# One UV tile for both halves of a paired chunk solve, and the chunk-end decay multiplied into the transposed keys

## The chip, the cores and the metric

One core of one Trainium2 chip. The metric is the device time of one execution in microseconds: the time from launch to end on that core. PE is TensorE, DVE is VectorE, ACT is ScalarE, POOL is GpSimd, SP is SyncE, whose queue only issues transfers.

## The reference, cut to what matters

One layer of a hybrid decoder, for a prompt of 2048 tokens and, with the same weights, for a decode step of 8 sequences by 4 tokens. One input projection feeds two token mixers; their gated outputs are merged and go through an output projection and a layer norm. The change is in the first mixer, a delta-rule recurrence with a state of 64x64 for each of 16 heads:

```python
def _rwkv7_recurrence(s0, r, w, k, v, kk, a):
    def step(s, inp):
        r_t, w_t, k_t, v_t, kk_t, a_t = inp
        s_kk = jnp.einsum('nhvk,nhk->nhv', s, kk_t)
        s = (s * w_t[:, :, None, :] - s_kk[..., None] * (kk_t * a_t)[:, :, None, :]
             + v_t[..., None] * k_t[:, :, None, :])
        return s, jnp.einsum('nhvk,nhk->nhv', s, r_t)
    xs = tuple(jnp.swapaxes(t, 0, 1) for t in (r, w, k, v, kk, a))
    s, y = lax.scan(step, s0, xs)
    return s, jnp.swapaxes(y, 0, 1)
...
    y_a = _norm(y_a, A_GN_EPS).reshape(n, t, A_WIDTH).astype(dt) * gn_a_gain + gn_a_bias
    o_a = (y_a + bonus.astype(dt)) * jax.nn.silu(z_a)
```

## The kernel before, in words

The prompt is cut into four segments of 512 tokens. In a segment the loop runs over four groups `h`, and a group holds two pairs of heads (`P0`, `P1`: a pair's 128 channels fill the partitions, 64 for each head). The large work is the projections: weight blocks `ww` against the segment's activations `uh` and `ul` (a high and a low part), matmuls `pp<-uh,ww` and `pp<-ul,ww` of 128x512 on PE, and the output projection `pp<-ww,mh` and `pp<-ww,ml`. The decode step is computed within the segment behind the second one.

A pair's 512 tokens are two halves of 256, and a half has C = 4 chunks of 64. `half` calls `prep`, which makes the tiles of a half: `AR` (scaled kk and r), `BK` (scaled a*kk and k), `UV` (for each head the values in one half of the partitions, and the state, later -U, in the other), `BT` (the transpose of `BK`, through a PSUM tile `sm`: the matmuls `sm<-cst,BK`), `W` (masked products of `BK` and `AR`, `sm<-AR,BK`), and `PL`, the decay of the state over a whole chunk (one number for each chunk and row). The step list `ORDER` has a `J` for each pair: first half, then `solve`, then second half. So one `solve` takes two halves together, the second half of one pair and the first half of the next, which do not depend on each other: 31 solves are of two halves and 2 of a single one (132 chunk steps, 124 of them paired).

`solve` inverts a triangular matrix for all chunks (tiles `ZX`, `HH`, `bdH`, `bdZ` in fp16, result `Z`), and then walks the four chunks in sequence. A chunk step is:

- X products, `ch<-UV,W` of 128x64: state and values against `W`; ScalarE copies X out (`tn<-ch`, the tile `xs`).
- Decayed state: ScalarE multiplies the state by `PL` (`tn<-UV,PL`, the tile `pst`), four instructions in a paired step (two heads by two halves).
- U products, `ch<-tn,Z`, and behind them in one bundle the first part of the output, `yy<-UV,AR`.
- Negation of U into `UV`, over the state that the two steps before have read: for each half one ScalarE instruction (head 0) and one VectorE instruction (head 1), `UV<-ch`.
- State products, `ch<-UV,BT` (S), and behind them in one bundle the second part of the output, `yy<-UV,W`.
- State update on VectorE: `UV[c+1] = S * PL + pst`, four scalar_tensor_tensor instructions (`UV<-ch,PL,tn`); at the last chunk the update goes to the state tile `sc`.

X, U and S lie in one PSUM tile `ch`, the output in `yy`. A bundle is a list of matmuls that PE does without anything between them.

No instruction is placed by hand. Each operation is recorded with its tiles by a helper (all rows of the profile have its line, L529, so the text goes by tile names), and a planner (`schedule`) fixes the order on each engine before the run: it keeps estimated durations (`cost`) and free tiles for each engine and always lets the engine that can start first take its next operation, by priority. On PE, `choose` prefers to stay with large matmuls or with small ones for some time (constants `STAY` 0.5 and `RUN` 2), since a change of shape costs time. The planner also keeps VectorE instructions with two inputs in SBUF and GpSimd instructions apart. The number of buffers of the tiles of a half is `JBN`, in the order `AR`, `W`, `UV`, `BT`, `Z`.

Of the kernel before, what the change touches and what calls it, by code (L numbers as in the profile page):

```python
# [25 lines left out]
C = JT // 64  # L26
# [38 lines left out]
DOFF = 0  # L65
JBN = 3, 2, 2, 2, 2
JB=dict(zip(("AR", "W", "UV", "BT", "Z"), JBN))
# [759 lines left out]
class Mixer:  # L827
# [227 lines left out]
    def ahead(self, n, g):  # L1055

        new = lambda tag: self.jb.tile([128, 512], F32R, tag=tag, name="w0", bufs=JB[tag])
        blk = FIRST[n]
        kw = {}
        if n == 2:  # L1060
            t = self.jb.tile([128, 2, 512], F32R, tag="W", name="w0", bufs=JB["W"])
            kw = dict(hi=t[:, 0], lo=t[:, 1])
        elif n == 3:
            kw = dict(hi=new("AR"), lo=new("BT"))
        elif n == 4:
            kw = dict(hi=new("UV"), lo=self.fx(dt=F32R))
        if not kw:
            if g == 0:
                self.wfirst[n] = self.ww.tile([128, 2, 2, 512], F32R, tag="ww", name="ww")
            kw = dict(hi=self.wfirst[n][:, g, 0], lo=self.wfirst[n][:, g, 1])  # L1070
        self.first[blk, g] = self.split(self.i["wf"][blk, g], **kw)
        if g == 0 and n > 2:
            self.early[blk] = (self.ch, self.yy)[n - 3].tile([128, 512], F32, tag=("ch", "yy")[n - 3], name="pp")
# [150 lines left out]
    def prep(self, s, p, j, slot, r, k, v, kn, g, lw):  # L1224
# [22 lines left out]
        self.act(P, cu, AF.Exp, scale=-0.5 * CDEC)  # L1247
        PL = self.jb.tile([128, C], F32, tag="PL", name="PL")
        G.tensor_copy(out=PL, in_=P[:, :, 64])
# [23 lines left out]

        UV = self.jb.tile([128, C, 2, 64], F32, tag="UV", name="UV", bufs=JB["UV"])
        ps = self.ps()
        pv = ps[:, 0:JT].rearrange("p (q t) -> p q t", q=2)
        self.pl.reserve = (UV,)
        for q in range(2):
            T.transpose(out=pv[:, q], in_=v2[:, q * 128:(q + 1) * 128], identity=self.ident)
        for e in range(2):  # L1280
            for h in range(2):
                A.copy(out=UV[64 - h * 64:128 - h * 64, e::2, h, :], in_=pv[e * 64:e * 64 + 64, :, h * 64:h * 64 + 64])

        ps = self.ps().rearrange("p (c t) -> p c t", c=C)
        for c in range(C):
            T.transpose(out=ps[:, c], in_=BK[:, c], identity=self.ident)
        BT = self.jb.tile([128, C, 128], F32, tag="BT", name="BT", bufs=JB["BT"])
        A.copy(out=BT, in_=ps)

# [4 lines left out]
        with self.pl.bundle():  # L1294
            for c in range(C):
                for h in range(2):
                    T.matmul(pw[h][:, c], lhsT=BK[HS[h], c], rhs=AR[HS[h], c], start=True, stop=True)
        B16, Bl, D = self.B16, self.bd["L"], slice(slot * C, (slot + 1) * C)
        for h in range(2):
# [4 lines left out]
            self.A.copy(out=W[R, h, :, 0:64], in_=AR[R, :, 0:64])  # L1304
        self.turns.append((p, AR, W, UV, BT, PL, bv, g[:, cs]))

    def half(self, s, p, j, ins):

        if not self.turns:
            self.B16 = self.j1.tile([128, 2 * C, 64], F16, tag="B16", name="B16")  # L1310
        self.prep(s, p, j, len(self.turns), *ins)

    def solve(self):
# [3 lines left out]
        ps_, self.turns = self.turns, []  # L1317
        Q = range(len(ps_))
        N = len(Q) * C
        B16, Bl, MB = self.B16[:, 0:N], self.bd["L"], self.bd["M"]  # L1320
# [54 lines left out]
        for c in range(C):  # L1375
            cp = self.ch.tile([128, 512], F32, tag="ch", name="ch").rearrange("p (k q t) -> p k q t", k=4, q=2)
            X, U, S = (cp[:, i, 0:len(Q)] for i in range(3))
            with self.pl.bundle():
                for q in Q:
                    p, AR, W, UV, BT, PL = ps_[q][:6]  # L1380
                    for h in range(2):
                        T.matmul(X[HS[h], q], lhsT=W[:, h, c, 0:64], rhs=UV[:, c, h], start=True, stop=True)
            xs = self.tiny(128).rearrange("p (q t) -> p q t", q=2)[:, 0:len(Q)]
            A.copy(out=xs, in_=X)
            pst = self.tiny(128).rearrange("p (q t) -> p q t", q=2)
            for q in Q:
                p, AR, W, UV, BT, PL = ps_[q][:6]
                for h in range(2):
                    R = HS[h]
                    self.act(pst[R, q], UV[R, c, h], AF.Copy, scale=PL[R, c:c + 1])  # L1390
            with self.pl.bundle():
                for q in Q:
                    for h in range(2):
                        T.matmul(U[HS[h], q], lhsT=Z[HS[h], q * C + c], rhs=xs[HS[h], q], start=True, stop=True)
                for q in Q:
                    p, AR, W, UV, BT, PL = ps_[q][:6]
                    for h in range(2):
                        T.matmul(Y[HS[h], q * C + c], lhsT=AR[HS[h], c, 64:128], rhs=UV[HS[h], c, h], start=q == 0, stop=False)
            for q in Q:
                UV = ps_[q][3]  # L1400
                self.act(UV[HS[0], c, 0], U[HS[0], q], AF.Copy, scale=-1.0)
                V.tensor_scalar(out=UV[HS[1], c, 1], in0=U[HS[1], q], scalar1=-1.0, scalar2=None, op0=MUL)
            with self.pl.bundle():
                for q in Q:
                    p, AR, W, UV, BT, PL = ps_[q][:6]
                    for h in range(2):
                        T.matmul(S[HS[h], q], lhsT=BT[:, c, HS[h]], rhs=UV[:, c, h], start=True, stop=True)
                for q in Q:
                    p, AR, W, UV, BT, PL = ps_[q][:6]
                    for h in range(2):  # L1410
                        T.matmul(Y[HS[h], q * C + c], lhsT=W[:, h, c, 64:128], rhs=UV[:, c, h], start=False, stop=q == len(Q) - 1)
            for q in Q:
                p, AR, W, UV, BT, PL = ps_[q][:6]
                if c < C - 1:
                    for h in range(2):
                        R = HS[h]
                        V.scalar_tensor_tensor(out=UV[R, c + 1, h], in0=S[R, q], scalar=PL[R, c:c + 1], in1=pst[R, q],
                                               op0=MUL, op1=ADD)
                else:
                    V.scalar_tensor_tensor(out=self.sc[:, p], in0=S[:, q], scalar=PL[:, c:c + 1], in1=pst[:, q],  # L1420
                                           op0=MUL, op1=ADD)
        yn = [self.groupnorm(Y[:, q * C:(q + 1) * C], C) for q in Q]
# [5 lines left out]
        for q in Q:  # L1428
            p, bv, g = ps_[q][0], *ps_[q][6:]
            t = self.t3()  # L1430
# [15 lines left out]
    def decode(self):  # L1446
# [94 lines left out]
        A.copy(out=BT, in_=ps)  # L1541
        UV = self.jb.tile([128, 8, 64], F32, tag="UV", name="UV", bufs=JB["UV"])
        self.pl.hold = self.pl.ops[-1]
# [496 lines left out]
```

## Time and profile before

| | us |
|---|---|
| median of 3 runs | 3134.05 |
| lowest, highest | 3130.12, 3137.01 |
| the profiled execution | 3128.51 |
| its span in the trace | 3126.7 |
| mean granted clock of TensorE, as a share of full speed | 0.969 |

The span runs from the first to the last instruction in the trace; the execution's time is 1.8 us longer. A time of this kernel compares with the median, and a sum over rows of the trace with the profiled execution.

### The profile page before, as it was taken

What the parts mean: (1) busy time and instruction counts of PE and PEld (TensorE: products, weight loads), DVE (VectorE), ACT (ScalarE), POOL (GpSimd) and SP (SyncE); (2) the same over time, 40 slices, a digit from 0 to 9 for tenths busy, and PEclk for the clock granted to TensorE, in tenths of its full rate; (3) what the DMA queues carried; (4) which work ended last, traced back from release to release, by engine and by line L of the source; (5) the groups of instructions that cost most, each with busy time, mean ns of one, the idle gap of its engine ahead of it and who ended that gap; (6) DMA issues with size and microseconds to landing.
All of it is one profiled execution on the core that took longest, in us unless ns stands there. A gap on an engine that the chain in (4) does not pass through costs nothing. (4 is left out here: it accounts for less than half of the span.)

```text
span 3126.7 us, 63842 instructions
## 1 busy us (share of the span) xinstructions
PE 2896.4 (93%) x24700; PEld 2332.8 (75%) x24700; DVE 1919.9 (61%) x4748; ACT 1566.2 (50%) x3859; POOL 1048.3 (34%) x1451
## 2 busy tenths in 40 slices
PE   8999999989989999989998788999999989998996
PEld 5777778768888989879774466777787766777675
DVE  3566676666576365565665575565676675566666
ACT  4466755656436455453541045554555346454652
POOL 4554456433252131222210242232232442334232
PEclk9999999999999999999998789999999999999997
DMA  8564556534362433425344432333343452533321
GB/s 303 199 229 161 175 191 222 191 127 160 117 226 99 130 108 112 137 94 178 136 128 150 158 110 97 135 124 122 131 152 124 156 176 79 172 119 122 108 83 38
DMA packets 132792, 451.86 MB, mean 145 GB/s; under 512 B 30500, under 2 KB 41636, under 8 KB 92680
## 3 DMA queue, kind: packets, MB, share of 16 engines
q0 software_dynamic: 33120, 241.19, 22.5%
q1 hardware_dynamic: 99368, 206.58, 19.6%
q8 instruction: 195, 3.19, 0.4%
q14 instruction: 109, 0.89, 0.1%
HBM read 345.83 MB, written 101.88 MB: 143 GB/s over the span
## 5 line engine op out<-in xcount | busy, mean ns | idle before, releaser
L529 PE MATMUL pp<-uh,ww 128*128 128x512 f32 (+1 forms) x5152 | 1476.8, 366 | 43.8 <-DMA ww<-wc_wf 15.6
L529 PEld LDWEIGHTS pp<-uh,ww 128*128 128x128 f32 x5152 | 880.5, 190 | 168.3 <-DVE t L529 22.7
L529 PE MATMUL pp<-ul,ww 128*128 128x512 f32 (+1 forms) x2576 | 883.7, 364 | 0.1
L529 PEld LDWEIGHTS pp<-ul,ww 128*128 128x128 f32 x2576 | 468.6, 190 | 54.5 <-issue 1.4
L529 POOL DMA_DIRECT2D ww<-wc_wf x190 | 109.0, 574 | 625.3 <-PE pp L529 514.5
L529 POOL TENSOR_TENSOR ww<-fx,ww 128x512 fp32r<-128x512 f32 x178 | 234.4, 1330 | 211.5 <-ACT ww L529 197.7
L529 ACT CAST ZX<-sm 128x512 f16<-128x512 f32 (+1 forms) x363 | 206.3, 572 | 91.0 <-PE sm L529 86.7
L529 ACT ACTIVATE tn<-UV,PL 64x64 f32<-64x64 f32 x512 | 177.0, 346 | 117.9 <-DVE UV L529 95.8
L529 POOL TENSOR_TENSOR t<-t,t 128x256 fp32r<-128x256 f32 (+2 forms) x160 | 150.6, 943 | 199.5 <-ACT t L529 189.1
L529 DVE TENSOR_TENSOR HH<-sm,lev 128x512 f16<-128x512 f32 (+1 forms) x165 | 111.3, 674 | 160.5 <-PE sm L529 159.7
L529 PE MATMUL pp<-ww,mh 128*128 128x256 f32 x960 | 190.4, 290 | 3.5 <-ACT zt L529 1.9
L529 DVE TENSOR_SCALAR UV<-ch 64x64 f32<-64x64 f32 x256 | 55.2, 227 | 207.3 <-ACT UV L529 184.4
L529 POOL TENSOR_TENSOR tn<-tn,mhalf 128x4 f32<-128x4 f32 (+2 forms) x108 | 100.9, 935 | 216.1 <-DVE tn L529 214.1
L529 PE MATMUL pp<-ww,uh 128*128 128x256 f32 x1024 | 171.6, 291 | 1.4 <-DVE t L529 0.8
L529 ACT CAST bdZ<-sm 64x512 f16<-64x512 f32 (+1 forms) x264 | 149.5, 566 | 24.9 <-PE sm L529 20.1
L529 PEld LDWEIGHTS pp<-ww,mh 128*128 128x128 f32 x960 | 154.9, 193 | 8.0 <-ACT zt L529 2.3
L529 PEld LDWEIGHTS pp<-ww,uh 128*128 128x128 f32 x1024 | 140.7, 190 | 5.3 <-ACT UV L529 0.7
L529 DVE SCALAR_TENSOR_TENSOR UV<-ch,PL,tn 64x64 f32<-64x64 f32 x384 | 108.7, 283 | 57.4 <-PE ch L529 47.5
L529 ACT ACTIVATE t<-pp 128x512 f32<-128x512 f32 (+1 forms) x160 | 80.6, 519 | 118.3 <-PE pp L529 100.7
L529 PE MATMUL pp<-ww,ml 128*128 128x256 f32 x480 | 138.4, 289 | 0.1
L529 ACT ACTIVATE UV<-ch 64x64 f32<-64x64 f32 x256 | 51.6, 215 | 171.3 <-PE yy L529 137.8
L529 DVE COPY bdH<-HH 64x512 f16<-64x512 f16 (+1 forms) x396 | 124.7, 315 | 8.5
(255 smaller groups left out, 5420.1 us busy)
## 6 DMA issues: line engine op xcount, KB each, us to landing
ww<-wc_wf POOLq DMA_DIRECT2D x190, 1024.0 KB, 5.1
wc_wf<-ww SPq DMA_DIRECT2D x65, 1024.0 KB, 5.4
fx<-in_wf SPq DMA_DIRECT2D x140, 256.0 KB, 3.4
ww<-wc_wv POOLq DMA_DIRECT2D x24, 1024.0 KB, 5.2
ww<-wc_wo POOLq DMA_DIRECT2D x16, 1024.0 KB, 5.1
wa<-in_wa SPq DMA_DIRECT2D x16, 512.0 KB, 5.2
wc_wv<-ww SPq DMA_DIRECT2D x8, 1024.0 KB, 5.5
fx<-in_wo SPq DMA_DIRECT2D x32, 256.0 KB, 2.8
```

Of the source, the lines that this page charges most:

```text
L529: op.fn = lambda: real(*[res(x) for x in a], **{k: res(x) for k, x in kw.items()})
```

## The change

It has four parts.

- `UV` and `PL` are no longer made for each half: `half` makes one tile of each for the two halves of a solve, `[128, 2, C, 2, 64]` and `[128, 2, C]`, and `prep` fills its slot. One `UV` tile takes the place of two (`JBN` 2 to 1). In the decode step the tile that was called `UV` comes from another pool, and so does one early weight block that borrowed the space.
- In `prep`, behind the products of `BK` and `AR`, VectorE multiplies `BK` in place by `PL` (128x512, one instruction a half). The transposes to `BT` are moved behind that, so that `BT` holds the decay.
- In `solve` the decayed state `pst` is made by VectorE, one 64x128 product for each head and both halves. The negation of U is one ScalarE and one VectorE instruction for both halves. The state update is then S + `pst`, one 64x128 addition for each head.
- With a single half the same instructions have 64 columns.

```diff
-JBN = 3, 2, 2, 2, 2
+BKG = 0
+PSG = 0
+JBN = 3, 2, 1, 2, 2
...
         elif n == 4:
-            kw = dict(hi=new("UV"), lo=self.fx(dt=F32R))
+            if g == 0:
+                self.wfirst[n] = self.jb.tile([128, 2, 512], F32R, tag="UV", name="w0", bufs=JB["UV"])
+            kw = dict(hi=self.wfirst[n][:, g], lo=self.fx(dt=F32R))
...
-        PL = self.jb.tile([128, C], F32, tag="PL", name="PL")
+        PL = self.PL[:, slot]
         G.tensor_copy(out=PL, in_=P[:, :, 64])
...
-        UV = self.jb.tile([128, C, 2, 64], F32, tag="UV", name="UV", bufs=JB["UV"])
+        UV = self.UV[:, slot]
...
-        self.pl.reserve = (UV,)
+        if slot == 0:
+            self.pl.reserve = (self.UV,)
...
-        ps = self.ps().rearrange("p (c t) -> p c t", c=C)
-        for c in range(C):
-            T.transpose(out=ps[:, c], in_=BK[:, c], identity=self.ident)
-        BT = self.jb.tile([128, C, 128], F32, tag="BT", name="BT", bufs=JB["BT"])
-        A.copy(out=BT, in_=ps)
...
                     T.matmul(pw[h][:, c], lhsT=BK[HS[h], c], rhs=AR[HS[h], c], start=True, stop=True)
+        (G if BKG else V).tensor_tensor(out=BK, in0=BK, in1=PL.unsqueeze(2).broadcast_to([128, C, 128]), op=MUL)
+        ps = self.ps().rearrange("p (c t) -> p c t", c=C)
+        for c in range(C):
+            T.transpose(out=ps[:, c], in_=BK[:, c], identity=self.ident)
+        BT = self.jb.tile([128, C, 128], F32, tag="BT", name="BT", bufs=JB["BT"])
+        A.copy(out=BT, in_=ps)
...
         if not self.turns:
             self.B16 = self.j1.tile([128, 2 * C, 64], F16, tag="B16", name="B16")
+            self.UV = self.jb.tile([128, 2, C, 2, 64], F32, tag="UV", name="UV", bufs=JB["UV"])
+            self.PL = self.jb.tile([128, 2, C], F32, tag="PL", name="PL")
...
+        UVs, PLs = self.UV[:, 0:len(Q)], self.PL[:, 0:len(Q)]
...
-            pst = self.tiny(128).rearrange("p (q t) -> p q t", q=2)
-            for q in Q:
-                p, AR, W, UV, BT, PL = ps_[q][:6]
-                for h in range(2):
-                    R = HS[h]
-                    self.act(pst[R, q], UV[R, c, h], AF.Copy, scale=PL[R, c:c + 1])
+            pst = self.tiny(128).rearrange("p (q t) -> p q t", q=2)[:, 0:len(Q)]
+            for h in range(2):
+                R = HS[h]
+                (G if PSG else V).tensor_tensor(out=pst[R], in0=UVs[R, :, c, h],
+                                                in1=PLs[R, :, c:c + 1].broadcast_to([64, len(Q), 64]), op=MUL)
...
-            for q in Q:
-                UV = ps_[q][3]
-                self.act(UV[HS[0], c, 0], U[HS[0], q], AF.Copy, scale=-1.0)
-                V.tensor_scalar(out=UV[HS[1], c, 1], in0=U[HS[1], q], scalar1=-1.0, scalar2=None, op0=MUL)
+            self.act(UVs[HS[0], :, c, 0], U[HS[0]], AF.Copy, scale=-1.0)
+            V.tensor_scalar(out=UVs[HS[1], :, c, 1], in0=U[HS[1]], scalar1=-1.0, scalar2=None, op0=MUL)
...
-            for q in Q:
-                p, AR, W, UV, BT, PL = ps_[q][:6]
-                if c < C - 1:
-                    for h in range(2):
-                        R = HS[h]
-                        V.scalar_tensor_tensor(out=UV[R, c + 1, h], in0=S[R, q], scalar=PL[R, c:c + 1], in1=pst[R, q],
-                                               op0=MUL, op1=ADD)
-                else:
-                    V.scalar_tensor_tensor(out=self.sc[:, p], in0=S[:, q], scalar=PL[:, c:c + 1], in1=pst[:, q],
-                                           op0=MUL, op1=ADD)
+            if c < C - 1:
+                for h in range(2):
+                    R = HS[h]
+                    V.tensor_tensor(out=UVs[R, :, c + 1, h], in0=S[R], in1=pst[R], op=ADD)
+            else:
+                for q in Q:
+                    V.tensor_tensor(out=self.sc[:, ps_[q][0]], in0=S[:, q], in1=pst[:, q], op=ADD)
```

Since the planner places every operation anew, the order on all engines changes. Over the whole program PE turns between large matmuls (128x256 and 128x512) and all others 2713 times before, 2601 times with the change; PE has the same number of matmuls. Three places on PE follow. In the rows a matmul is named by output<-inputs, its shape and how many stand in a row.

The first place is a paired chunk step in the middle of the program, from the U products to the next X products. Before:

```order
L529 MATMUL ch<-tn,Z 64x64 x4
L529 MATMUL yy<-UV,AR 64x64 x4
L529 MATMUL pp<-uh,ww 128x512 x2
L529 MATMUL ch<-UV,BT 64x64 x4
L529 MATMUL yy<-UV,W 64x64 x4
L529 MATMUL pp<-ul,ww 128x512
L529 MATMUL pp<-uh,ww 128x512 x2
L529 MATMUL pp<-ul,ww 128x512
L529 MATMUL ch<-UV,W 64x64 x4
```

With the change:

```order
L531 MATMUL ch<-tn,Z 64x64 x4
L531 MATMUL yy<-UV,AR 64x64 x4
L531 MATMUL pp<-ul,ww 128x512
L531 MATMUL pp<-uh,ww 128x512
L531 MATMUL ch<-UV,BT 64x64 x4
L531 MATMUL yy<-UV,W 64x64 x4
L531 MATMUL pp<-uh,ww 128x512
L531 MATMUL pp<-ul,ww 128x512
L531 MATMUL pp<-uh,ww 128x512
L531 MATMUL ch<-UV,W 64x64 x4
```

Two large matmuls stand between the U and the S products as before; between the S products and the next X products there are three instead of four.

The second place is the end of the decode step's state products, `sm<-d,BT`, where `d` is a temporary tile of the decode step (its number tells the tiles apart). Before:

```order
L529 MATMUL sm<-d_21554,BT 64x256 x2
L529 MATMUL sm<-d_21567,BT 64x256 x2
L529 MATMUL sm<-d_21574,BT 64x256 x2
...
L529 MATMUL sm<-d_21627,BT 64x256 x2
L529 MATMUL sm<-cst,t_20695 128x128 x2
L529 MATMUL sm<-d_21637,BT 64x256 x2
L529 MATMUL sm<-d_21657 32x32 x4
```

With the change:

```order
L531 MATMUL sm<-d_21184,BT 64x256 x2
L531 MATMUL pp<-uh,ww 128x512 x2
L531 MATMUL pp<-ul,ww 128x512
L531 MATMUL pp<-uh,ww 128x512 x2
L531 MATMUL pp<-ul,ww 128x512
L531 MATMUL sm<-d_21209,BT 64x256 x2
L531 MATMUL pp<-uh,ww 128x512 x2
L531 MATMUL pp<-ul,ww 128x512
L531 MATMUL sm<-d_21219,BT 64x256 x2
```

The last state products stood in a row of their own and now stand between large matmuls. In the whole stretch from the first of them to `sm<-d 32x32` there are 42 large matmuls before and 158 with the change, the last 61 of them behind the last state product.

The third place is in the last paired solve of the program. Before, one chunk step from its S products on:

```order
L529 MATMUL ch<-UV,BT 64x64 x4
L529 MATMUL yy<-UV,W 64x64 x4
L529 MATMUL pp<-ww,mh 128x256
L529 MATMUL pp<-ww,ml 128x256
L529 MATMUL pp<-ww,mh 128x256 x2
L529 MATMUL pp<-ww,ml 128x256
L529 MATMUL pp<-ww,mh 128x256 x2
L529 MATMUL pp<-ww,ml 128x256
L529 MATMUL pp<-ww,mh 128x256
L529 MATMUL ch<-UV,W 64x64 x4
```

With the change, from the S products of its first step on:

```order
L531 MATMUL ch<-UV,BT 64x64 x4
L531 MATMUL yy<-UV,W 64x64 x4
L531 MATMUL pp<-ww,ml 128x256
L531 MATMUL pp<-ww,mh 128x256
L531 MATMUL ch<-UV,W 64x64 x4
L531 MATMUL ch<-tn,Z 64x64 x4
L531 MATMUL yy<-UV,AR 64x64 x4
L531 MATMUL ch<-UV,BT 64x64 x4
L531 MATMUL yy<-UV,W 64x64 x4
L531 MATMUL ch<-UV,W 64x64 x4
```

From the second step on the small matmuls follow each other with nothing between, and the last half's `sm<-AR,BK`, which stood behind this solve, stands ahead of these steps.

## Rows read from the trace of the kernel before

**Rows 1.** The page: busy time, share of the span and instructions of each engine.

```profile
PE 2896.4 (93%) x24700; PEld 2332.8 (75%) x24700; DVE 1919.9 (61%) x4748; ACT 1566.2 (50%) x3859; POOL 1048.3 (34%) x1451
```

**Rows 2.** Groups by shape: busy us, mean ns, idle before, what ended it.

```profile
L529 PE MATMUL ch<-UV,W 128*64 128x64 f32 x1024 | 60.4, 235 | 11.9 <-DVE UV L529 4.5 <-ACT W L529 3.0
...
L529 PE MATMUL ch<-UV,BT 128*64 128x64 f32 x1024 | 59.2, 235 | 36.4 <-DVE UV L529 34.6 <-ACT UV L529 1.4
```

**Rows 3.** Waits: who waited for whom, us in total, times, longest.

```profile
DVE UV L529 <- ACT UV L529: 184.4, 180, 2.6
...
PE ch L529 <- DVE UV L529: 39.1, 97, 1.3
...
PE sm L529 <- DVE BK L529: 19.6, 6, 11.1
```

**Rows 4.** Timeline of one paired chunk step: start us, us, work, idle before.

```profile
1919.00 0.45 PE L529 MATMUL ch<-UV,W 128*64 128x64 f32 x8
...
1920.58 0.45 PE L529 MATMUL ch<-tn,Z 64*64 64x64 f32 x8
...
1920.86 0.40 PE L529 MATMUL yy<-UV,AR 64*64 64x64 f32 x8
...
1921.23 0.22 ACT L529 ACTIVATE UV<-ch 64x64 f32<-64x64 f32 x1 [0.97 <-PE yy L529]
...
1921.48 0.23 DVE L529 TENSOR_SCALAR UV<-ch 64x64 f32<-64x64 f32 x1 [2.54 <-ACT UV L529]
...
1921.81 0.22 ACT L529 ACTIVATE UV<-ch 64x64 f32<-64x64 f32 x1 [0.35 <-DVE UV L529]
1922.05 0.23 DVE L529 TENSOR_SCALAR UV<-ch 64x64 f32<-64x64 f32 x1 [0.34 <-ACT UV L529]
...
1922.34 0.45 PE L529 MATMUL ch<-UV,BT 128*64 128x64 f32 x8 [0.41 <-DVE UV L529]
...
1922.84 1.23 DVE L529 SCALAR_TENSOR_TENSOR UV<-ch,PL,tn 64x64 f32<-64x64 f32 x4 [0.56 <-PE ch L529]
...
1924.21 0.45 PE L529 MATMUL ch<-UV,W 128*64 128x64 f32 x8 [0.28 <-DVE UV L529]
```

**Rows 5.** Groups by shape on ScalarE and VectorE: instructions that go, and nearest prices.

```profile
L529 ACT ACTIVATE tn<-UV,PL 64x64 f32<-64x64 f32 x512 | 177.0, 346 | 117.9 <-DVE UV L529 95.8 <-POOL PL L529 9.6 <-POOL t L529 2.0
...
L529 DVE SCALAR_TENSOR_TENSOR UV<-ch,PL,tn 64x64 f32<-64x64 f32 x384 | 108.7, 283 | 57.4 <-PE ch L529 47.5
...
L529 DVE TENSOR_TENSOR W<-sm,cst 128x512 f32<-128x512 f32 x129 | 84.8, 679 | 16.2 <-PE sm L529 15.8
...
L529 ACT COPY UV<-sm 64x128 f32<-64x128 f32 x256 | 66.4, 260 | 20.9 <-PE sm L529 17.6
...
L529 DVE TENSOR_TENSOR t<-t,t 128x512 f32<-128x512 f32 x24 | 19.2, 800 | 0.5
...
L529 DVE TENSOR_TENSOR d<-d,roped 64x128 f32<-64x128 f32 x4 | 1.1, 286 | 0.1
```

**Rows 6.** Timeline of PE: large matmuls and eight small ones between them.

```profile
2059.50 0.39 PE L529 MATMUL pp<-uh,ww 128*128 128x512 f32 x1
2059.73 0.41 PE L529 MATMUL sm<-HH,bdZ 128*128 128x64 f16 x8
2059.97 0.48 PE L529 MATMUL pp<-uh,ww 128*128 128x512 f32 x1
2060.29 0.39 PE L529 MATMUL pp<-ul,ww 128*128 128x512 f32 x1
```

**Rows 7.** Timeline of PE: the decode step's state products, first row and what follows.

```profile
1671.58 0.38 PE L529 MATMUL sm<-d,BT 64*64 64x256 f32 x1
...
1709.92 0.61 PE L529 MATMUL sm<-d 128*32 128x32 f32 x8 [4.89 <-DVE d L529]
```

**Rows 8.** Windows: length; busy (x) of PE, PEld, DVE, ACT, POOL; PEclk, DMA, GB/s.

```profile
1690.00:1700.00 10.00, 5.26 (x22) 1.73 (x24) 5.90 (x17) 0.00 (x0) 0.00 (x0) 0.60 0.63 215
1700.00:1710.00 10.00, 4.50 (x20) 1.51 (x17) 7.38 (x23) 2.36 (x8) 0.00 (x0) 0.50 0.48 165
```

More of the change, by code (lines that the diff above doesn't have):

```diff
@@ L1304, in prep @@
             self.A.copy(out=W[R, h, :, 0:64], in_=AR[R, :, 0:64])
-        self.turns.append((p, AR, W, UV, BT, PL, bv, g[:, cs]))
+        self.turns.append((p, AR, W, UV, BT, bv, g[:, cs]))
     def half(self, s, p, j, ins):
@@ L1379, in solve @@
                 for q in Q:
-                    p, AR, W, UV, BT, PL = ps_[q][:6]
+                    p, AR, W, UV, BT = ps_[q][:5]
                     for h in range(2):
@@ L1395, in solve @@
                 for q in Q:
-                    p, AR, W, UV, BT, PL = ps_[q][:6]
+                    p, AR, W, UV, BT = ps_[q][:5]
                     for h in range(2):
                         T.matmul(Y[HS[h], q * C + c], lhsT=AR[HS[h], c, 64:128], rhs=UV[HS[h], c, h], start=q == 0, stop=False)
-            for q in Q:
-                UV = ps_[q][3]
-                self.act(UV[HS[0], c, 0], U[HS[0], q], AF.Copy, scale=-1.0)
-                V.tensor_scalar(out=UV[HS[1], c, 1], in0=U[HS[1], q], scalar1=-1.0, scalar2=None, op0=MUL)
+            self.act(UVs[HS[0], :, c, 0], U[HS[0]], AF.Copy, scale=-1.0)
+            V.tensor_scalar(out=UVs[HS[1], :, c, 1], in0=U[HS[1]], scalar1=-1.0, scalar2=None, op0=MUL)
             with self.pl.bundle():
                 for q in Q:
-                    p, AR, W, UV, BT, PL = ps_[q][:6]
+                    p, AR, W, UV, BT = ps_[q][:5]
                     for h in range(2):
@@ L1408, in solve @@
                 for q in Q:
-                    p, AR, W, UV, BT, PL = ps_[q][:6]
+                    p, AR, W, UV, BT = ps_[q][:5]
                     for h in range(2):
                         T.matmul(Y[HS[h], q * C + c], lhsT=W[:, h, c, 64:128], rhs=UV[:, c, h], start=False, stop=q == len(Q) - 1)
-            for q in Q:
-                p, AR, W, UV, BT, PL = ps_[q][:6]
-                if c < C - 1:
-                    for h in range(2):
-                        R = HS[h]
-                        V.scalar_tensor_tensor(out=UV[R, c + 1, h], in0=S[R, q], scalar=PL[R, c:c + 1], in1=pst[R, q],
-                                               op0=MUL, op1=ADD)
-                else:
-                    V.scalar_tensor_tensor(out=self.sc[:, p], in0=S[:, q], scalar=PL[:, c:c + 1], in1=pst[:, q],
-                                           op0=MUL, op1=ADD)
+            if c < C - 1:
[5 more added lines that the diff above has]
+                    V.tensor_tensor(out=self.sc[:, ps_[q][0]], in0=S[:, q], in1=pst[:, q], op=ADD)
         yn = [self.groupnorm(Y[:, q * C:(q + 1) * C], C) for q in Q]
@@ L1428, in solve @@
         for q in Q:
-            p, bv, g = ps_[q][0], *ps_[q][6:]
+            p, bv, g = ps_[q][0], *ps_[q][5:]
             t = self.t3()
@@ L1541, in decode @@
         A.copy(out=BT, in_=ps)
-        UV = self.jb.tile([128, 8, 64], F32, tag="UV", name="UV", bufs=JB["UV"])
+        UV = self.t5((128, 8, 64))
         self.pl.hold = self.pl.ops[-1]
```

## The prediction

> **What bounds the kernel now.** I read the engines' busy shares first, then the groups by shape, then the waits, and last two stretches of the timeline. The shares [rows 1] make PE the bound: busy 2896.4 us, 93% of the span, with VectorE at 61% and ScalarE at 50%. So only two things can shorten the span: time in which PE's queue stands at a matmul whose input is late, and time lost when PE turns from one shape to another. The change touches the chunk chain, four small steps per solve that run beside the large projections. Of its matmuls the state products (`ch<-UV,BT`) have 36.4 us of PE idle in front of them, 34.6 of it for VectorE's `UV`; the next chunk's first products (`ch<-UV,W`) have 11.9, of which 4.5 for that reason [rows 2]. The waits agree: 39.1 us in 97 waits of `ch` for VectorE's `UV`, the largest sum on PE itself, and VectorE in turn sat 184.4 us behind ScalarE's `UV` [rows 3].
>
> One paired chunk step shows why [rows 4]. The U products start at 1920.58. Then ScalarE negates U of the first half at 1921.23, VectorE at 1921.48, ScalarE the second half's at 1921.81, VectorE at 1922.05: four instructions strictly in turn, although they write disjoint places. Only then does PE start the state products, at 1922.34, after 0.41 us of idling. VectorE's four state updates take 1.23 us more (from 1922.84), and the next chunk's first products start at 1924.21. The matmuls that stand between as cover were too few for the first of these waits.
>
> **The change, part by part.**
>
> *Negation of U.* Four instructions per paired step become two. The 64x64 ones take 0.22 on ScalarE and 0.23 on VectorE [rows 4]. A 64x128 copy from PSUM takes 260 ns on ScalarE; for VectorE I take 0.29, from the 286 ns of a 64x128 product [rows 5]. Against this, one negation now serves both halves and must wait for the last of the Y products, not for the first half's: they end at 1921.26 (1920.86 and 0.40), and ScalarE started at 1921.23 [rows 4]. So: start 1921.33, ScalarE to 1921.59, VectorE 1921.62 to 1921.91, PE at 1921.97 instead of 1922.34. That is 0.37 of the 0.41 idle us. In the built order the cover between U and S stays about as it was, two large matmuls at the commonest place (first place of the order), so the wait shrinks by nine tenths at best: 31 us of 34.6. Some steps have less cover than before; I take 28, bounds 15 and 34.6.
>
> The Trainium skill (Perfetto Trace Analysis, Optimizing Scalar/DVE Operations) speaks against this: where ScalarE and VectorE aren't saturated but cause bubbles elsewhere, it advises breaking instructions up so that work completes sooner. By that rule the merge would lengthen the wait. Here the pieces ran in turn and PE waited for the last of them anyway [rows 4], so the trace disagrees; a result of that kind is among the rivals.
>
> *State update.* Four scalar_tensor_tensor (283 ns each [rows 5], 1.23 us in a row [rows 4]) become two additions of 64x128 at about 0.3: 0.6 us. The next step's products may start 0.63 us sooner; PE idled only 4.5 us there [rows 2], and I take all 4.5 (bounds 0 and 11.9). The order takes one large matmul out of that cover, which the 0.63 us pays for.
>
> *Decayed state.* 512 ScalarE instructions of 346 ns, 177.0 us [rows 5], go; 264 VectorE products of 64x128 at 286 ns [rows 5] come, 75 us. They stand behind the additions, while PE does the X products, ScalarE copies X out and PE comes to the U products: 1.58 us in the step shown (1919.00 to 1920.58 [rows 4]) against 0.57 for two of them, so they cost nothing; without any cover between X and U they still fit under the X products (0.45) and the copy of X. ScalarE copies X out sooner: 1 us.
>
> *Decay into the keys.* 64 new VectorE products of 128x512 in place. Their price lies between 679 ns (one input in PSUM) and 800 ns (both in SBUF) [rows 5]; I take 800, the same operands: 51 us of VectorE, hidden while PE is the bound. What is queued behind: the masks of `W`, so the solve's lead-in is 0.8 us later, under projections. Who waits: PE's transposes of `BK`, moved behind the product. In the built order at least 4 large matmuls stand between, 13 or more at half of the 64 places, which covers about 0.9 us (0.8 and two hand-overs of some 0.05). PE already waits for `BK` 19.6 us, in 6 waits, longest 11.1 [rows 3]; that wait passes to the first matmul that reads `BK`. I charge 4 us, bounds 0 and 20.
>
> VectorE in sum: 108.7 us of updates [rows 5] and 256 negations at 0.23 [rows 4], 59 us, give way to 186 additions and 124 negations at some 0.29, 90 us; with 75 and 51 it gains about 48 us, 61% to 63%. ScalarE loses 177 and 256 times 0.22 and takes back 124 times 0.26: 201 us less.
>
> *Re-planned order.* All engines' instructions are placed anew. Two things in it can be priced. Turns between large matmuls and all else fall from 2713 to 2601. A large matmul begins 0.23 us before what follows (2059.50 to 2059.73); the one behind eight small ones takes 0.32 (2059.97 to 2060.29) [rows 6]. So one excursion loses about 0.09 us there, and 56 fewer are worth 5 us (bounds 0 and 11, twice that).
>
> Second place of the order: the decode step's state products (`sm<-d,BT`), from 1671.58 to 1709.92 [rows 7], had 42 large matmuls among them and then none; PE was busy 5.26 and 4.50 of 10 us in two windows, at a granted clock of 0.60 and 0.50 [rows 8], in the second the lower of the two levels (1.2 GHz), after PE had stood idle for half of the first. In the new order 158 stand there. That is 116 more at 0.23, 27 us of work; the last 61 of them take 14 us where the old order left 4.89 us of idling [rows 7], so the stretch grows by 9. Gain 18 us (bounds 0 and 28, the latter if that stretch doesn't grow and some of the clock comes back).
>
> Third place: the last paired solve stands later, and three of its four steps have no cover at all. Such a step takes 1.39 from U to S by the sum above, 1.24 from S to the next X (0.50 to the updates, 0.6 for them, 0.14 to PE [rows 4]) and at most 1.58 from X to U: about 4 us against 5.21 today (1919.00 to 1924.21), with PE idle for over half of it; the large matmuls that stood there come elsewhere, and the last half's `AR,BK` products come ahead. I take 0 (bounds -3, a us less per step, and +9, three us per step that nothing gives back).
>
> Sum: -28 -4.5 -1 +4 -5 -18 +0 = -52.5 us. The profiled execution took 3128.5 us, so 3076; the median shown is 3134.05, 5.5 above it. For the median of the changed kernel I say **3081 us**. Its own range is 3055 to 3100.
>
> **The rivals.**
>
> *The stalls only move* (0.14). PE's order is fixed before the run with estimated durations; a chain that is faster by 1 us per step is planned tighter, with less cover, and waits just as long: the order does take a large matmul out of the cover between S and X. Then the chain's 33.5 us are lost and half of the other 19: 3134 - 10 = 3124; with nothing left, 3134. For it: the planner stands between every saving and PE. Against: the one wait that is large came from four instructions in turn.
>
> *The transposes of `BK` wait* (0.10, the slower side). If the product is late on VectorE, PE's queue stands at the transposes, 64 times. Each needs to be 0.88 us late on average to eat the gain (52.5 and the 4 charged, over 64). With 1.2 us it is 77: 3081 + 73 (4 are charged) = 3154. For it: `BK` is already the second of PE's own waits [rows 3]. Against: 13 large matmuls at half the places.
>
> *VectorE and GpSimd in each other's way* (0.10). A 128x512 product with both inputs in SBUF takes 800 ns, with one in PSUM 679 [rows 5]; GpSimd is 34% busy [rows 1]. New VectorE products with both inputs there last 126 us (75 and 51); if GpSimd is held for all of it, and a quarter of that comes before a matmul for which PE waits, 31 us are lost: 3112. Against: none of PE's larger waits in the rows is for GpSimd. The Trainium skill (SBUF — State Buffer, SBUF: two separate sides) describes such a lock between the two engines, held for a whole instruction; no row here isolates it.
>
> *The merged negation is only later* (0.04). If the pieces of a half already overlapped with PE's work, the merge would add the 64 further columns on each engine (0.04 and 0.06) and the wait for the last Y product (0.1): 128 steps would lose 26 us where I gain 28, 3081 + 54 = 3135. Against it stand the four pieces in turn [rows 4].
>
> *More than that* (0.12). The decode term at its bound, all of the chain's idling, and fewer half-clock stretches: 3040.
>
> The forecast itself has 0.50. A fifth of a per cent, 6 us, is about what a measurement of this kernel can tell from no change. Faster by more: forecast 0.49, the lock 0.09, the larger gain 0.12, the first rival 0.09: 0.79. Within: 0.08. Slower: the transposes 0.10 and 0.03 of the others: 0.13. The range of eight in ten: 3035 to 3130; it leaves out the transposes, the far end of the gain and part of the unchanged cases.
>
> **What would show it.** PE's idle before `ch<-UV,BT` falls from 36.4 us to under 10, and before `ch<-UV,W` to under 8; VectorE's wait for ScalarE's `UV` falls by half or more; a paired step with cover shows one ScalarE and one VectorE negation in turn. VectorE near 1970 busy us, ScalarE near 1365. The idle before `sm<-cst,BK` stays under 25 us. The decode products are followed by large matmuls at the full clock. I am wrong if the idle before `ch` stays above 30 us, if the transposes wait in dozens of places, or if new stalls at other tiles take back what these gave.

## The result, and the profile after

The changed kernel takes 3090.32 us (median of 4 runs, 3086.27 to 3091.8) against 3134.44 for the kernel before (median of 4 runs): a ratio of 0.9859, 95% interval 0.9841 to 0.9876, 44 us faster. The forecast was 3081 us, with its own range 3055 to 3100. The span of the profiled execution falls from 3126.7 to 3087.4 us, by 39.3, and PE's idle time by 42.4: 230.3 us before (3126.7 less 2896.4 [rows 1]), 187.9 after. PE's own work is about as long as it was (2896.4 and 2899.5).

The page of the changed kernel, then its groups by shape and its waits, which answer to [rows 2, 3, 5]:

```profile
PE 2899.5 (94%) x24700; PEld 2345.6 (76%) x24700; DVE 1976.0 (64%) x4766; ACT 1369.3 (44%) x3223; POOL 1060.8 (34%) x1451
```

```profile
L531 PE MATMUL sm<-AR,BK 64*128 64x128 f32 x1024 | 91.4, 291 | 19.8 <-DVE BK L531 14.5 <-DVE Z L531 2.4 <-DVE t L531 1.9
L531 DVE TENSOR_TENSOR tn<-UV,PL 64x128 f32<-64x128 f32 x248 | 86.8, 350 | 8.7 <-POOL PL L531 1.2 <-ACT UV L531 0.6
...
L531 PE MATMUL ch<-UV,W 128*64 128x64 f32 x1024 | 61.5, 239 | 10.8 <-DVE UV L531 5.6 <-ACT W L531 5.0
L531 PE MATMUL ch<-UV,BT 128*64 128x64 f32 x1024 | 60.7, 240 | 9.9 <-DVE UV L531 7.7 <-ACT UV L531 0.8
...
L531 DVE TENSOR_TENSOR UV<-ch,tn 64x128 f32<-64x128 f32 x186 | 53.6, 288 | 50.8 <-PE ch L531 47.5
L531 DVE TENSOR_TENSOR BK<-BK,PL 128x512 f32<-128x512 f32 x64 | 50.2, 784 | 28.4 <-PE sm L531 28.1
...
L531 PE MATMUL sm<-cst,BK 128*128 128x128 f32 x256 | 44.1, 281 | 5.1 <-DVE W L531 2.8 <-ACT UV L531 1.3 <-DVE BK L531 0.4
```

```profile
DVE UV L531 <- ACT UV L531: 150.7, 106, 3.2
...
PE sm L531 <- DVE BK L531: 15.1, 5, 13.5
...
PE ch L531 <- DVE UV L531: 13.3, 24, 0.9
```

PE's waits for the decode step's `d`, before and with the change:

```profile
PE sm L529 <- DVE d L529: 12.0, 10, 4.9
...
PE sm L529 <- ACT d L529: 3.2, 4, 2.3
```

```profile
PE sm L531 <- DVE d L531: 0.7, 3, 0.3
...
PE sm L531 <- ACT d L531: 0.4, 1, 0.4
```

The idle before the state products falls from 36.4 to 9.9 us, in front of the next X products from 11.9 only to 10.8, and the part of the latter that ends with VectorE's `UV` rises from 4.5 to 5.6. PE's wait for VectorE's `UV` falls from 97 times to 24. VectorE still waits 150.7 us for ScalarE's `UV`, so the two negations still run in turn; with one of each that costs PE little. Two signs that the forecast named did not come: this wait did not fall by half (from 184.4, and from 180 times to 106), and the idle before the X products is not under 8 us. The transposes `sm<-cst,BK` hardly wait (5.1); 15.1 us for `BK` stand now nearly all before `sm<-AR,BK`, 13.5 of them in one place. Added up over all their rows, PE's waits fall from 209.0 to 168.6 us, by 40.4. The chain's `UV` (39.1 to 13.3) and the decode step's `d` (15.2 to 1.1) make 39.9 of that; all the others, some up and some down by as much as 11 us, cancel.

One paired step of the changed kernel, timeline, as in [rows 4]:

```profile
1900.99 0.45 PE L531 MATMUL ch<-tn,Z 64*64 64x64 f32 x8
...
1901.70 0.27 ACT L531 ACTIVATE UV<-ch 64x128 f32<-64x128 f32 x1 [4.96 <-PE yy L531]
...
1902.01 0.29 DVE L531 TENSOR_SCALAR UV<-ch 64x128 f32<-64x128 f32 x1 [0.21 <-ACT UV L531]
1902.36 0.45 PE L531 MATMUL ch<-UV,BT 128*64 128x64 f32 x8
...
1902.86 0.61 DVE L531 TENSOR_TENSOR UV<-ch,tn 64x128 f32<-64x128 f32 x2 [0.56 <-PE ch L531]
...
1903.49 0.60 DVE L531 TENSOR_TENSOR tn<-UV,PL 64x128 f32<-64x128 f32 x2
...
1903.88 0.45 PE L531 MATMUL ch<-UV,W 128*64 128x64 f32 x8
```

From U to the state products it is 1.37 us where it was 1.76, with no idle on PE; from there to the next X products 1.52 where it was 1.87, with one large matmul less between.

### The profile page after: what moved, and what is told of

It reads as the page before. It is cut to its first block, busy times and chain, and to the rows that moved or that the text cites. A ratio compares the mean times of both kernels' runs of the same rounds, so it can differ in the third digit from the quotient of the medians.

```text
span 3087.4 us, 62919 instructions
## 1 busy us (share of the span) xinstructions
PE 2899.5 (94%) x24700; PEld 2345.6 (76%) x24700; DVE 1976.0 (64%) x4766; ACT 1369.3 (44%) x3223; POOL 1060.8 (34%) x1451
## 4 chain that ended last, share of the span: by engine, by line
PE 70%; DVE 13%; ACT 9%; issue 3%; DMA 2%; POOL 2%; SPq 0%; DVEq 0%; POOLq 0%; ACTq 0%
PE pp L531 49%; PE sm L531 14%; PE ch L531 5%; ACT t L531 3%; DVE t L531 3%; ACT UV L531 2%; DVE tn L531 2%; PE yy L531 2%; DVE zt L531 2%; DVE BK L531 1%; ACT L531 1%; DVE bdH L531 1%; DVE HH L531 1%; DVE W L531 1%; DVE AR L531 1%
## 5 line engine op out<-in xcount | busy, mean ns | idle before, releaser
L531 DVE COPY bdH<-HH 64x512 f16<-64x512 f16 (+1 forms) x396 | 146.9, 371 | 6.8 <-PE sm L531 0.3
L531 DVE TENSOR_SCALAR UV<-ch 64x128 f32<-64x128 f32 (+1 forms) x132 | 38.3, 290 | 156.5 <-ACT UV L531 150.7
L531 ACT COPY tn<-ch 128x128 f32<-128x128 f32 (+1 forms) x132 | 34.6, 262 | 230.2 <-PE ch L531 230.1
L531 ACT CAST ww<-fx 128x512 fp32r<-128x512 f32 x178 | 105.1, 621 | 40.9 <-PE pp L531 19.8
L531 ACT ACTIVATE UV<-ch 64x128 f32<-64x128 f32 (+1 forms) x132 | 35.3, 267 | 196.5 <-PE yy L531 196.3
```

Source lines behind the costliest of these rows:

```text
L531: op.fn = lambda: real(*[res(x) for x in a], **{k: res(x) for k, x in kw.items()})
```

## The experiments

**The order of the matmuls kept.** The planner places everything anew after any edit. To see what the instructions alone do, four kernels hold the sequence of all 24700 matmuls of the changed kernel (PE takes the next one of a written list), while the other engines are planned around it. Each puts back a part of the old chain in the new tiles. The list and its use in the planner, and the edit of p_neg4:

```diff
+        pin = [pes[i] for i in pin]
...
-                    k = self.choose(av, pe, st)
+                k = [x[2] for x in av].index(pin[pos])
...
-            self.act(UVs[HS[0], :, c, 0], U[HS[0]], AF.Copy, scale=-1.0)
-            V.tensor_scalar(out=UVs[HS[1], :, c, 1], in0=U[HS[1]], scalar1=-1.0, scalar2=None, op0=MUL)
+            for q in Q:
+                self.act(UVs[HS[0], q, c, 0], U[HS[0], q], AF.Copy, scale=-1.0)
+                V.tensor_scalar(out=UVs[HS[1], q, c, 1], in0=U[HS[1], q], scalar1=-1.0, scalar2=None, op0=MUL)
```

In p_nodecay the product into the keys goes and the old update returns; in p_pstact the decayed state alone is made as before; p_old_chain has all three edits.

```diff
-        (G if BKG else V).tensor_tensor(out=BK, in0=BK, in1=PL.unsqueeze(2).broadcast_to([128, C, 128]), op=MUL)
...
+                        V.scalar_tensor_tensor(out=UVs[R, q, c + 1, h], in0=S[R, q], scalar=PLs[R, q, c:c + 1], in1=pst[R, q],
+                                               op0=MUL, op1=ADD)
```

```diff
+                    self.act(pst[R, q], UVs[R, q, c, h], AF.Copy, scale=PLs[R, q, c:c + 1])
```

p_old_chain, expected: 

> The changed kernel's order of all matmuls is kept, and the chunk chain is put back to its old instructions (four negations in turn, decayed state on ScalarE, scalar_tensor_tensor updates, no product into the keys). If the gain comes from the shorter chain, it goes: PE's idle before the state products returns to 30 us or more, and the time is 3120 to 3145 us (over the old one is possible, since one large matmul less covers the way from S to X). If the gain comes from the new order of the matmuls (the decode step, fewer turns), the time stays at 3085 to 3100 us.

p_neg4, expected: 

> The changed kernel's order of all matmuls is kept, and only the negation of U is cut into four instructions again. By the forecast's term the idle before the state products rises by some 26 us, to 33 to 40 us, and the time to 3110 to 3120 us. If the merge matters little, because the products behind it were late for another reason, it stays below 3097 us.

p_nodecay, expected: 

> The changed kernel's order of all matmuls is kept; the product into the keys is left out and the state update is four scalar_tensor_tensor instructions again. By the forecast's terms (4.5 us gained at the next X products, 4 us lost at the keys) nothing moves: 3086 to 3096 us. If the saved 0.6 us of each update is what allowed the order to take a large matmul out of that stretch, the idle before the X products rises from 10.8 to 40 us or more and the time to 3115 to 3135 us.

p_pstact, expected: 

> The changed kernel's order of all matmuls is kept, and only the decayed state is made by four ScalarE instructions again. By the forecast's term of 1 us: 3088 to 3096 us, with VectorE 87 us less busy and ScalarE 177 us more. If the negation of U then queues behind them on ScalarE, the idle before the state products rises over 15 us and the time over 3098 us.

Measured: p_old_chain 3206.24 us (ratio to before 1.0223, 1.0203 to 1.0244), p_neg4 3130.74 (0.9987, 0.9978 to 0.9997), p_nodecay 3138.71 (1.0007, 0.9998 to 1.0017), p_pstact 3137.77 (1.0011, 1.0001 to 1.0022). p_old_chain and p_neg4 lost more than was expected. p_pstact took its second branch. p_nodecay came near its second branch, 4 us above that range and with 35.5 us of idle where 40 were said. Their groups for the X and the state products, in this sequence:

```profile
L534 PE MATMUL ch<-UV,W 128*64 128x64 f32 x1024 | 62.3, 241 | 35.4 <-DVE UV L534 30.5 <-ACT W L534 4.7
L534 PE MATMUL ch<-UV,BT 128*64 128x64 f32 x1024 | 61.9, 244 | 51.4 <-DVE UV L534 50.4 <-ACT UV L534 0.7
```

```profile
L534 PE MATMUL ch<-UV,W 128*64 128x64 f32 x1024 | 62.4, 240 | 11.2 <-ACT W L534 5.9 <-DVE UV L534 5.1
L534 PE MATMUL ch<-UV,BT 128*64 128x64 f32 x1024 | 61.1, 241 | 46.9 <-DVE UV L534 45.1 <-ACT UV L534 1.6
```

```profile
L534 PE MATMUL ch<-UV,W 128*64 128x64 f32 x1024 | 61.6, 238 | 35.5 <-DVE UV L534 30.6 <-ACT W L534 4.7
L534 PE MATMUL ch<-UV,BT 128*64 128x64 f32 x1024 | 60.6, 240 | 11.4 <-DVE UV L534 9.0 <-ACT UV L534 0.9
```

```profile
L534 PE MATMUL ch<-UV,W 128*64 128x64 f32 x1024 | 61.8, 240 | 10.6 <-DVE UV L534 5.6 <-ACT W L534 4.8
L534 PE MATMUL ch<-UV,BT 128*64 128x64 f32 x1024 | 61.4, 242 | 16.4 <-DVE UV L534 11.0
```

Each part costs its own wait when it is undone: the negation 37.0 us before the state products (9.9 to 46.9), the update 24.7 us before the X products (10.8 to 35.5), and at most 1.5 at the other's place. So the order alone does not bring the gain: in this order the old chain is 116 us slower, and 72 us slower than the kernel before. The order is tighter than the old one, which mostly had four large matmuls between S and X. The reverse, the new instructions in the old order, was not run, nor the changed kernel with the list and no other edit. p_neg4, whose 40 us are nearly its own wait, leaves little for the list itself.

For the negation that wait is nearly the whole loss. For the update it is half of 48 us, and the rest was not followed. The decayed state is the surprise: 47 us, of which only 6.5 show before the state products. The page of that run:

```profile
PE 2919.7 (93%) x24700; PEld 2358.2 (75%) x24700; DVE 1888.2 (60%) x4502; ACT 1545.2 (49%) x3735; POOL 1056.8 (34%) x1451
```

PE is idle for 221.0 us (3140.7 less 2919.7), 33 more than in the changed kernel, in rises of a few us each at many tiles; and its busy time is 20 us longer, at a mean granted clock of 0.960 where the changed kernel had 0.966. ScalarE is 176 us busier there, VectorE 88 less; PE's waits, added up over that view's rows, rise from 63 to 79 us for ScalarE and from 90 to 108 for VectorE. How a busier ScalarE makes VectorE's results late was not followed further.

**Single parts, placed anew.** In `e_dec` the decode step's `UV` comes from the other pool, nothing else; `e_neg` adds the pair tile and the merged negation; `e_decay` is the kernel before with the product into the keys behind the matmuls of `BK` and `AR`, and additions of 64x64, four a step; `a_old_chain` is the changed kernel with the old chain, the edits of `p_old_chain` without the list. The edit of e_dec, and the line of e_decay that takes the place of the scalar_tensor_tensor:

```diff
-        UV = self.jb.tile([128, 8, 64], F32, tag="UV", name="UV", bufs=JB["UV"])
+        UV = self.t5((128, 8, 64))
```

```diff
+                        V.tensor_tensor(out=UV[R, c + 1, h], in0=S[R, q], in1=pst[R, q], op=ADD)
```

e_dec, expected: 

> The kernel before with one edit: the decode step's tile that was called UV comes from the other pool, as in the changed kernel, and the planner places everything anew. In its order 173 large matmuls instead of 42 stand among and behind the decode step's state products, and the cover in the chunk steps is as before. By the forecast's decode term (18 us): 3110 to 3122 us, with the idle before the state products of the chunk chain still at 34 to 39 us. If the decode step costs the same wherever these matmuls stand: 3128 to 3138 us.

e_neg, expected: 

> The edit of the run before this one, and the UV tile for two halves with the merged negation; decayed state, updates and keys as before the change. By the forecast's terms (18 and 28 us): 3083 to 3096 us, with the idle before the state products under 12 us. If a chain that is planned shorter only gets less cover: that idle stays over 25 us and the time is 3105 to 3120 us.

e_decay, expected: 

> The kernel before with the decay multiplied into the keys alone (transposes behind it, updates as additions of 64x64, four in a row; negations, tiles and decayed state as before), placed anew. In its order the way from S to the next X has mostly 3 large matmuls where it had 4, and the decode products 108 where they had 42. By the forecast's terms the keys cost 4 us, the updates gain little (four short additions are still some 1 us), decode gains some 10: 3122 to 3132 us. If the transposes wait for VectorE: 3140 us or more.

a_old_chain, expected: 

> The changed kernel's tiles (one UV and PL for two halves, the decode step's tile moved) with the chunk chain's old instructions, placed anew by the planner, which it was not in the run that kept the order. If a longer chain is only given its cover back, most of the 116 us that it cost in the kept order go: 3105 to 3125 us, with the idle before the state products at 30 to 40 us. If the short instructions are worth 100 us in any order: 3180 us or more.

Measured: e_dec 3138.6 us (1.0015, 1.0006 to 1.0024), e_neg 3137.0 (1.0008, 0.9999 to 1.0018), e_decay 3160.16 (1.0089, 1.0068 to 1.0111), a_old_chain 3168.14 (1.0116, 1.0096 to 1.0136). No part alone gains anything; all four times lie above what the forecast's terms gave. e_dec came out within 1 us of its second branch; e_decay's time is that of late transposes, but they were not late; a_old_chain lies between its two branches.

For e_dec the waits before the state products and `sm<-d` of the decode step are gone, but new ones stand ahead of them. PE's timeline of e_dec:

```profile
1614.27 1.22 PE L529 MATMUL sm<-d,bones 128*128 128x256 f32 x2 [2.87 <-ACT d L529]
...
1625.05 1.22 PE L529 MATMUL sm<-d,bones 128*128 128x256 f32 x2 [7.85 <-DVE d L529]
```

That is 10.7 us of idle at the head of the decode step, before a group that never waits in the kernel before or in the changed one. The tile's pool is the same in e_dec and in the changed kernel; where the large matmuls stand was the planner's choice.

For e_neg the merged negation does much of what it did in the whole change, 36.0 to 13.9 us; the X products lose 9 (11.9 to 20.8). First e_dec's line, then e_neg's:

```profile
L529 PE MATMUL ch<-UV,BT 128*64 128x64 f32 x1024 | 59.0, 235 | 36.0 <-DVE UV L529 34.2 <-ACT UV L529 1.4
```

```profile
L529 PE MATMUL ch<-UV,W 128*64 128x64 f32 x1024 | 61.8, 238 | 20.8 <-DVE UV L529 13.2 <-ACT W L529 2.2
L529 PE MATMUL ch<-UV,BT 128*64 128x64 f32 x1024 | 61.1, 241 | 13.9 <-DVE UV L529 8.6 <-ACT UV L529 0.4
```

But two solves of this order have three steps each with no large matmul in them, and there PE works and waits in turn at a lower clock. Timeline of PE, and windows, of e_neg:

```profile
2628.01 0.70 PE L529 MATMUL ch<-UV,BT 128*64 128x64 f32 x8 [0.74 <-DVE UV L529]
2628.49 0.64 PE L529 MATMUL yy<-UV,W 128*64 128x64 f32 x8
2630.12 0.70 PE L529 MATMUL ch<-UV,W 128*64 128x64 f32 x8 [1.00 <-DVE UV L529]
2631.23 0.69 PE L529 MATMUL ch<-tn,Z 64*64 64x64 f32 x8 [0.41 <-ACT tn L529]
```

```profile
2620.00:2640.00 20.00, 11.80 (x162) 9.73 (x159) 6.06 (x22) 6.39 (x21) 0.19 (x1) 0.50 0.01 2
...
3040.00:3060.00 20.00, 12.02 (x164) 9.49 (x163) 6.24 (x19) 5.75 (x18) 0.00 (x0) 0.54 0.00 1
```

These are forty microseconds at a granted clock of 0.50, the lower of the two levels, and 0.54, with PE busy for six tenths of them. In the profiled executions the busy time of PE itself rises from 2902.0 us in e_dec to 2916.1, which is more than the 8.7 us of idle that the merge takes away in all (230.8 to 222.1, spans 3132.8 and 3138.2).

a_old_chain against the changed kernel is the chain's instructions with the planner free in both: 3168.14 less 3090.32, 78 us. Against the kernel before it is the tiles, the moved transposes and a new order: 34 us lost. At a border of segments PE is idle for 32 us almost in one piece, where the changed kernel's longest wait for `BK` is 13.5:

```profile
1809.97 1.21 PE L531 MATMUL sm<-cst,t 128*128 128x128 f32 x4 [11.35 <-DVE t L531]
1831.59 1.11 PE L531 MATMUL sm<-cst,BK 128*128 128x128 f32 x4 [20.41 <-DVE BK L531]
```

The planner gave the old chain back 38 of the 116 us. In e_decay the transposes are not late (4.5 us before `sm<-cst,BK`), but 34.4 us stand before `sm<-AR,BK`, 26.8 of them for `BK`, and 48.4 before the state products, the wait that nothing in it removes.

**Is the gain a lucky order?** Two planner constants that bear on nothing but the order, each in both kernels:

```diff
-WIN = 500
+WIN = 450
...
-DL = 2.55
+DL = 2.6
```

c_before_win450, expected: 

> The kernel before with the planner's constant WIN at 450 instead of 500, which bears on nothing but the order. It shows how far a new order alone moves the time. If the gain of the change is that of its instructions: this one within 15 us of 3134 us, and its pair with the change some 30 to 45 us below it. If the measured 44 us are a lucky order: either of the pair moves by 20 us or more, and the distance of the two is under 20 us.

c_after_win450, expected: 

> The changed kernel with WIN at 450, the other half of the pair. Gain of the instructions: 3085 to 3105 us. A lucky order before: 3110 us or more.

c_before_dl26, expected: 

> The kernel before with the planner's estimate of a transfer's latency, DL, at 2.6 instead of 2.55, a second pair of the same kind. Gain of the instructions: within 15 us of 3134 us. If the order decides: 20 us or more away from it in either direction.

c_after_dl26, expected: 

> The changed kernel with DL at 2.6. Gain of the instructions: 30 to 45 us below its pair, 3085 to 3105 us. If the order decides: 3110 us or more.

Measured: WIN 450 3145.82 and 3107.85, DL 2.6 3138.09 and 3092.84 (ratios to the kernel before 1.0046, 0.9921, 1.0012 and 0.9875; intervals 1.003 to 1.0062, 0.9894 to 0.9947, 0.9999 to 1.0026, 0.9856 to 0.9895). Three of the four came as expected; the changed kernel with WIN 450 came 3 us above its range. A new order alone moves either kernel by 2 to 18 us; the pairs lie 38 and 45 us apart, beside 44 for the original pair. So the gain of the whole change does not hang on one lucky order. The idle before the state products goes with the change each time, as in [rows 2] (with DL 2.6 it is 38.6 and 10.0 us); WIN 450 without and with it:

```profile
L529 PE MATMUL ch<-UV,BT 128*64 128x64 f32 x1024 | 60.2, 238 | 43.2 <-DVE UV L529 42.8
```

```profile
L531 PE MATMUL ch<-UV,BT 128*64 128x64 f32 x1024 | 60.4, 239 | 9.8 <-DVE UV L531 7.5 <-ACT UV L531 0.8
```

## Why the prediction held, step by step

*Negation: right.* Forecast -28 us of the 34.6, measured 26.5 of idle (36.4 to 9.9). The two instructions take 0.27 and 0.29 us as taken, and U to S 1.37 us where the sum said 1.39. The Trainium skill's advice to break instructions up (Perfetto Trace Analysis, Optimizing Scalar/DVE Operations) does not help here: with the order kept, the four short ones cost PE 37 us.

*State update: mis-sized.* The additions take 288 ns and the pair 0.61 us, as forecast. But of the 4.5 us only 1.1 came as idle time before the X products, and the part that was meant, the wait for VectorE's `UV`, rose by 1.1 (4.5 to 5.6). The order had spent the saving, with three large matmuls where four stood: with the order kept the update is worth 24.7 us of idle there.

*Decayed state: right that VectorE hides it, wrong on two sizes.* The updates that need it wait for the state products (47.5 of 50.8 us), not for it. The product takes 350 ns, not 286, 87 us in all. And "1 us" for ScalarE's release is too small: with the order kept, moving these 176 us back to ScalarE cost 47 us, mostly outside the chain and by a way that stays open.

*Keys: right on the price (784 ns against 800), wrong sign.* Instead of 4 us lost, PE's wait for `BK` fell from 19.6 to 15.1 us, and it moved to the first reader as said. That, too, belongs to this order: in e_decay, with the same product, the first reader waits 26.8 us for `BK`. The rival of late transposes falls: 5.1 us.

*Decode: right on the stretch, but it doesn't carry to the whole.* The stretch from the first state product to `sm<-d` grew from 38.3 us to 49.2 (1651.15 to 1700.31) with 116 more large matmuls in it, 27 us of work: 16 us gained, 18 forecast. Windows of the changed kernel, beside [rows 8]:

```profile
1660.00:1690.00 30.00, 30.00 (x141) 16.82 (x141) 18.66 (x49) 2.57 (x4) 3.10 (x7) 1.00 0.68 221
1690.00:1720.00 30.00, 27.96 (x106) 17.01 (x104) 12.24 (x31) 2.49 (x6) 1.82 (x5) 0.83 0.64 215
```

In e_dec the same stretch, with 131 more, took 50.78 us (1668.53 to 1719.31), which by the same count is 18 gained, and yet its time did not fall: 10.7 us went at the head of the decode step, the rest was not followed. So what the stretch gives the program depends on the order, and the tile's move does not bring it by itself.

*Fewer turns: not shown.* No run isolates the 5 us.

*Last solve: mis-sized.* Taken as 0. PE's timeline of one of its steps without cover, in the changed kernel:

```profile
3005.99 0.45 PE L531 MATMUL ch<-UV,W 128*64 128x64 f32 x8 [0.57 <-DVE UV L531]
3006.85 0.69 PE L531 MATMUL ch<-tn,Z 64*64 64x64 f32 x8 [0.41 <-ACT tn L531]
...
3008.64 0.69 PE L531 MATMUL ch<-UV,BT 128*64 128x64 f32 x8 [0.68 <-DVE UV L531]
...
3010.14 0.70 PE L531 MATMUL ch<-UV,W 128*64 128x64 f32 x8 [0.38 <-DVE UV L531]
```

```profile
3015.00:3045.00 30.00, 22.54 (x138) 16.59 (x138) 18.23 (x67) 13.62 (x41) 4.33 (x5) 0.57 0.05 18
```

A step takes 4.15 us as said. But the matmuls, once PE has only short ones and waits in turn, are slower from 3006.85 on (0.69 instead of 0.45 for eight in a row), and the window from 3015 to 3045 was granted 0.57 of the clock. If each matmul is counted by the median distance to the next one for its shape in both kernels, the last 82 us of such work took 126 us before and 139 after: 13 us lost, over the bound of 9. Counted over the last 200 us the loss is 6 (262 and 268), so part of it may come back in the work ahead, where the large matmuls went.

By the profiled executions (3128.51 and 3089.27) 39.2 us came of the sum's 52.5. Of the 13 that lack, the last solve is 6 to 13, the update 3.4, the negation 1.5 and decode 2, less the 8.5 by which the keys were better: 4 to 11. Other places moved too and the turns were not measured, so this is an account and no proof. By the medians the forecast is 9 us off. That errors of this size in both directions left so little is in part luck.

*The rival of the lock* between VectorE and GpSimd left no mark on PE: its waits that end with GpSimd add up to 10.1 us before and 2.5 with the change, and GpSimd's busy time rises by 12.5 us only. No run isolates it.

*The rival "the stalls only move"* is half true: the tighter order did eat the update's saving, and a chain that is long again gets cover back. It does not eat the negation's. What the forecast did not see is that its terms cannot be had one by one: e_neg, with both terms that were priced highest, was put at 3083 to 3096 us and took 3137. The sum came out near for the order at hand, which the forecast had read, not because each edit is worth its term. Why the planner leaves some solves without cover in one order and not in another was not tried.

## What to carry to other kernels

Where several short instructions run in turn on two engines and a third waits for the last, merge them over an independent axis; the place to see it is the wait for the last, and the proof is a run that keeps the order and puts them back. Where a scheduler stands between an edit and the time, price the edit in the order that it yields, and run a pair or two with a neutral constant changed before a difference of under 1% is believed. Look in the new order for stretches without large matmuls: in those shown here PE ran at a granted clock of 0.50 to 0.57, and in e_neg PE's longer busy time took back more than the merge had saved in idle.

## What was not expected of the hardware

A scalar_tensor_tensor of 64x64 with a scalar column took 283 ns [rows 5], an addition of twice as many columns 288. A 64x128 product of the state and `PL`, whose one number is repeated along the row, took 350, where 286 stood for one of the same size [rows 5], which repeats rows of 32. What makes the difference was not tried.
